# Thirty-six matmuls of a constant tile into an unused PSUM bank, at the head of a decoder layer

## The chip, the cores and the metric

The kernel runs on one NeuronCore of a Trainium2 chip. The metric is device time in microseconds of one execution, from the first to the last instruction with what lies around them. Five engines run their own instruction streams: PE (TensorE, matmuls; its weight loads are listed apart as PEld), DVE (VectorE), ACT (ScalarE), POOL (GpSimd) and SP, which here only issues DMAs.

## What is computed

One decoder layer over 512 tokens of width 1024, all in 32-bit floats: an RMS norm, one wide projection, two attention branches, a mixture of experts, an embedding gate and a final norm. Cut to what the change stands beside, the head of it:

```python
h = _rmsnorm(x, attn_norm[i])
proj = jnp.matmul(h, w_in[i])
q_a, c_kv, q_idx, k_idx, w_idx, qkv_b, gate_a, gate_b = _split_cols(proj)
...
rel = jax.nn.relu(jnp.einsum("bqhe,bse->bqhs", qi, k_idx))
score = jnp.einsum("bqhs,bqh->bqs", rel, wi)
_, idx = lax.top_k(score, n_sel)
...
x = x + jnp.matmul(merged, w_out[i])
x = x + _hier_moe(_rmsnorm(x, ffn_norm[i]), ...)
x = x + jnp.matmul(p[i], w_ple[i]) * jax.nn.sigmoid(jnp.matmul(_rmsnorm(x, ple_norm[i]), w_ple_gate[i]))
return _rmsnorm(x, final_norm)
```

## The kernel before

Tokens lie in four tiles `xs[0]` to `xs[3]` of 128 rows by 1024 columns. Each is loaded by one DMA from SP's queue (L102). ACT's queue loads `ident`, the 128x128 identity (L105), and then the norm gains, four small DMAs into the 32-row tile `norms` (L108 to L111). DVE fills `ones_r`, a 128x128 tile of ones, among its first instructions (L122).

PE's order is the order of the code, since PE is scheduled by hand; the other engines' orders come from a scheduler, and `pin` ties some instructions to the one traced ahead of them. PE's first instruction is a transpose of `norms` into bank 1 (`gains_ps`, L215). Meanwhile each x tile goes through ACT (sum of squares, L220), DVE and POOL (reciprocal root, L125 and L126) and DVE (scaling of the tile, L222).

Then x is turned: `turn_x(t, k)` (L232) transposes the 128x128 block k of tile t into column range t of bank `tps[k]`. For the first three tiles and k = 0 to 6 these are 21 transposes. The fourth tile is turned block by block inside `split_x(k)`: a transpose on PE, then ACT copies the bank, scaled by the gain, into the high half `hT_hi` (L132), and DVE writes the rest as `hT_lo` (L136). The last block, k = 7, has no bank of its own and follows when bank 2 has been read. High and low halves feed every projection as three matmuls (`mm3`, L80 to L82), first the key index `kidx_ps`, then the query index `qidx_ps`. Weights go through the same kind of split: POOL writes `whi` (L130), DVE `wlo` (L134).

PSUM has eight banks. `tps` takes 2, 3, 4, 5, 6, 7 and 0, in this order; bank 1 holds `gains_ps` and after it `kidx_ps`. Bank 0 is first written by the transposes of block 6.

The lines around the place of the change:

```python
gp_ = bank(1, "gains_ps")
nc.tensor.transpose(gp_[:, :32], norms, ident[:32, :32])
ss = cp.tile([P, 4], F32, name="ss1")
for t in range(NT):
...
for t in range(NT - 1):
    for k in range(len(tps)):
        turn_x(t, k)
wki = take("ki", ahead=0)
```

Of the kernel before, what the change touches and what calls it, by code (L numbers as in the profile page):

```python
# [18 lines left out]
P = 128  # L19
# [30 lines left out]
def hybrid_layer_kernel(ctx: ExitStack, tc: tile.TileContext, x, p, attn_norm, w_in, kv_norm, w_uk, w_uv,  # L50
                        rel_bias, w_branch_a, w_branch_b, w_out, ffn_norm, w_r1, b_r1, w_r2, b_r2,
                        w_gate, w_up, w_down, ple_norm, w_ple_gate, w_ple, final_norm, cst, out):
    nc = tc.nc
# [6 lines left out]
    def bank(i, name):  # L60
        return ps.tile([P, S], F32, tag=f"bank{i}", bufs=1, name=name)
# [59 lines left out]
    negtri, strict_r, ones_r = [cp.tile([P, P], F32R, name=n) for n in ("negtri", "strict_r", "ones_r")]  # L121
# [91 lines left out]

    gp_ = bank(1, "gains_ps")
    nc.tensor.transpose(gp_[:, :32], norms, ident[:32, :32])  # L215
    ss = cp.tile([P, 4], F32, name="ss1")
    for t in range(NT):
        xt = xs[t]
# [700 lines left out]
    for u in range(NT):  # L919
        n = NT - u  # L920
        nc.tensor.matmul(rkp[:, (u + 1) * NE:(NT + 1) * NE], ones_r, hits[:, u:u + 1, :].to_broadcast([P, n, NE]),
                         start=False, stop=u == NT - 1, skip_group_check=True)
# [360 lines left out]
```

## Time and profile before

| | us |
|---|---|
| median of 3 runs | 761.29 |
| lowest and highest of the 3 | 759.28, 762.74 |
| the profiled execution | 756.49 |
| its span, first to last instruction | 754.8 |
| PE busy in the span | 723.3 |

The profiled execution has 1.7 us around its span. Start times below are counted from the start of the span. A matmul's row starts where it starts and its end is modelled, so neighbours overlap: what one of a row of equal matmuls costs is the distance of the starts, that is the stretch of the row less one duration, divided by their number less one. In the rows `xT_ps` and its kin are tiles by the program's names, and `x21` is the number of instructions that a row merges.

### The profile page before, as it was taken

How to read it: one execution, taken by the hardware profiler on the slowest of the kernel's cores; microseconds unless marked ns; L12 is line 12 of the kernel's file. 1: busy time of each engine (PE TensorE's matmuls, PEld its weight loads, DVE VectorE, ACT ScalarE, POOL GpSimd, SP SyncE). 2: the span in 40 equal slices, each digit the busy share in tenths (PEclk: the TensorE clock that was granted, in tenths of full speed). 3: DMA queues.
4: the chain of work that ended last, by engine and by line, in shares of the span. 5: the costliest groups of instructions: out<-in, count | busy, mean ns of one | idle time of the engine just before them, and what ended most of it. 6: DMA issues, size and time to landing. Idle time of an engine off the chain costs nothing. (4 is left out here: it accounts for less than half of the span.)

```text
span 754.8 us, 10213 instructions
## 1 busy us (share of the span) xinstructions
PE 723.3 (96%) x3696; PEld 506.7 (67%) x3696; DVE 452.9 (60%) x896; ACT 292.1 (39%) x657; POOL 216.7 (29%) x255
## 2 busy tenths in 40 slices
PE   5999999989999999999999999999999999998995
PEld 3889987867778778788878645444544445444885
DVE  5689999997877756326553513544555445545534
ACT  5364435535667554332212423222322222233723
POOL 3212323354462535124530221000100000217732
PEclk9999999999999999999999999999999999999999
DMA  7345332322222222287955669999999999995002
GB/s 241 93 139 159 85 85 56 98 85 84 84 71 85 70 84 85 84 239 265 367 175 230 214 225 377 410 414 410 407 411 402 406 383 412 402 364 196 1 1 111
DMA packets 89259, 160.59 MB, mean 213 GB/s; under 512 B 13497, under 2 KB 56562, under 8 KB 85106
## 3 DMA queue, kind: packets, MB, share of 16 engines
q1 hardware_dynamic: 78384, 150.78, 54.8%
q10 hardware_dynamic: 8514, 4.89, 2.2%
q0 software_dynamic: 2304, 4.20, 1.6%
q8 instruction: 31, 0.51, 0.3%
q14 instruction: 26, 0.21, 0.1%
HBM read 154.08 MB, written 9.96 MB: 217 GB/s over the span
## 5 line engine op out<-in xcount | busy, mean ns | idle before, releaser
L1031 PE MATMUL gu_ps<-ew,xT 128*64 128x512 f32 x512 | 112.9, 593 | 1.4 <-PEq L1073 1.3
L130 POOL TENSOR_SCALAR whi<-wraw 128x1024 fp32r<-128x1024 f32 (+1 forms) x51 | 56.4, 1106 | 138.7 <-issue 29.7
L1068 DVE TENSOR_TENSOR x<-cmb_ps,x 128x512 f32<-128x512 f32 x128 | 81.0, 682 | 12.5 <-PE cmb_ps L1066 12.5
L1031 PEld LDWEIGHTS gu_ps<-ew,xT 128*64 128x64 f32 x512 | 36.8, 137 | 74.2 <-issue 72.8
L134 DVE TENSOR_TENSOR wlo<-wraw,whi 128x1024 fp32r<-128x1024 f32 (+1 forms) x51 | 64.7, 1269 | 14.8 <-POOL whi L130 14.8
L1007 POOL DMA_INDIRECT xg<-h_d,trow x16 | 16.1, 1008 | 186.3 <-PE cmb_ps L1065 170.9
L1035 DVE TENSOR_TENSOR hid<-hid,gu_ps 128x256 f32<-128x256 f32 x16 | 6.8, 422 | 104.4 <-ACT hid L1034 104.4
L1054 PE MATMUL yp<-ew,hidT 128*64 128x512 f32 x256 | 58.7, 599 | 0.4 <-DVE hidT L1044 0.4
L80 PE MATMUL gate_ps<-hT_hi,whi 128*128 128x512 f32 x128 | 51.9, 405 | 2.4 <-DVE ks L297 1.8
L1065 PE MATMUL cmb_ps<-yh,hotT 128*128 128x512 f32 x128 | 53.1, 415 | 0.4 <-DVE h3T L1152 0.4
L132 ACT ACTIVATE yh<-yp,sm 128x512 fp32r<-128x512 f32 x32 | 22.0, 687 | 79.2 <-PE yp L1054 79.2
L81 PE MATMUL gate_ps<-hT_lo,whi 128*128 128x512 f32 x128 | 50.8, 397 | 0.0
L82 PE MATMUL gate_ps<-hT_hi,wlo 128*128 128x512 f32 x128 | 50.7, 396 | 0.0
L1066 PE MATMUL cmb_ps<-yl,hotT 128*128 128x512 f32 x128 | 50.4, 394 | 0.3 <-DVE yl L136 0.3
L1034 ACT ACTIVATE hid<-gu_ps 128x256 f32<-128x256 f32 x16 | 6.1, 383 | 97.3 <-PE gu_ps L1031 97.3
L1054 PEld LDWEIGHTS yp<-ew,hidT 128*64 128x64 f32 x256 | 16.9, 136 | 33.0 <-issue 28.1
L136 DVE SCALAR_TENSOR_TENSOR yl<-yp,sm,yh 128x512 fp32r<-128x512 f32 x32 | 24.0, 750 | 21.1 <-ACT yh L132 21.1
L1019 ACT ACTIVATE xT<-xg_ps,gpm 128x128 f32<-128x128 f32 x128 | 34.7, 383 | 3.8 <-PE xg_ps L1016 3.8
L583 ACT ACTIVATE px<-px,st 128x128 f32<-128x128 f32 (+3 forms) x32 | 17.8, 557 | 36.6 <-DVE st L582 36.5
L80 PEld LDWEIGHTS gate_ps<-hT_hi,whi 128*128 128x128 f32 x128 | 24.3, 190 | 9.1 <-POOL bm L562 3.6
L1065 PEld LDWEIGHTS cmb_ps<-yh,hotT 128*128 128x128 f32 x128 | 24.1, 188 | 6.9 <-issue 2.4
L82 PEld LDWEIGHTS gate_ps<-hT_hi,wlo 128*128 128x128 f32 x128 | 24.5, 191 | 5.5
(328 smaller groups left out, 1760.6 us busy)
## 6 DMA issues: line engine op xcount, KB each, us to landing
ew<-in_w_gate_dram SPq DMA_DIRECT2D x32, 1024.0 KB, 8.1
ew<-in_w_up_dram SPq DMA_DIRECT2D x32, 1024.0 KB, 8.5
ew<-in_w_down_dram SPq DMA_DIRECT2D x32, 1024.0 KB, 7.5
wraw<-in_w_in_dram SPq DMA_DIRECT2D x37, 512.0 KB, 3.7
gate_d<-gst ACTq DMA_DIRECT2D x16, 256.0 KB, 2.0
sg<-gate_d SPq DMA_DIRECT2D x16, 256.0 KB, 4.4
wraw<-in_w_out_dram SPq DMA_DIRECT2D x8, 512.0 KB, 7.3
wgraw<-in_w_ple_gate_dram SPq DMA_DIRECT2D x4, 1024.0 KB, 9.4
```

Of the source, the lines that this page charges most:

```text
L80: nc.tensor.matmul(o, lhs[0], rhs[0], start=first, stop=False)
L81: nc.tensor.matmul(o, lhs[0], rhs[1], start=False, stop=False)
L82: nc.tensor.matmul(o, lhs[1], rhs[0], start=False, stop=last)
L130: hold(nc.gpsimd.tensor_scalar(hi, raw, 1.0 if gain is None else gain, 1.0, op0=ALU.mult, op1=ALU.mult))
L134: hold(V.tensor_sub(lo, raw, hi.bitcast(F32)))
L136: hold(V.scalar_tensor_tensor(lo, raw, gain, hi.bitcast(F32), op0=ALU.mult, op1=ALU.subtract))
L1019: nc.scalar.activation(xT[half][:, k, :], tp[:, k * P:(k + 1) * P], AF.Copy, scale=gpm[:, kk:kk + 1])
L1031: nc.tensor.matmul(gu_ps[64 * e:64 * e + 64, :], xT[k // 4][:, k % 4, 64 * e:64 * e + 64], wq[i, k // 4][:, :, e * D + (k % 4) * 256:e * D ...
L1054: nc.tensor.matmul(yp[64 * e:64 * e + 64, :], hidT[:, k, 64 * e:64 * e + 64], wq[i, 2][:, e, k * D + nh * S:k * D + (nh + 1) * S], start=k ...
L1065: nc.tensor.matmul(cp_, hT_[:, t * P:(t + 1) * P], yh, start=True, stop=False)
L1066: nc.tensor.matmul(cp_, hT_[:, t * P:(t + 1) * P], yl, start=False, stop=True)
L1068: V.tensor_add(xd, cp_, xd)
```

## The change

Behind the transpose of the gains, a tile `idle_ps` is taken in bank 0, and 36 matmuls are issued into its first 128 columns, each with the tile of ones as weights and as moving operand. Nothing reads `idle_ps`.

```diff
     gp_ = bank(1, "gains_ps")
     nc.tensor.transpose(gp_[:, :32], norms, ident[:32, :32])
+
+    idle_ps = bank(0, "idle_ps")
+    for _ in range(36):
+        nc.tensor.matmul(idle_ps[:, :P], ones_r, ones_r, start=True, stop=True)
     ss = cp.tile([P, 4], F32, name="ss1")
     for t in range(NT):
         xt = xs[t]
```

On PE, at its very start, the order of before and after differ by this (the names are tiles; line numbers behind the insertion grow by 4):

```order
 L215 MATMUL gains_ps<-cst_sb,norms 128x32
-L232 MATMUL xT_ps<-cst_sb,xt 128x128 x28
+L219 MATMUL idle_ps<-ones_r 128x128 x36
+L236 MATMUL xT_ps<-cst_sb,xt 128x128 x28
 L80 MATMUL kidx_ps<-hT_hi,whi 72x512
 L81 MATMUL kidx_ps<-hT_lo,whi 72x512
```

The 36 stand between the transpose of the gains and the first 28 transposes of x; nothing else on PE moves. The same place of after, with the semaphores that each instruction waits on (DMAHW ones belong to DMAs, the others to engines):

```order
L215 MATMUL gains_ps<-cst_sb,norms 128x32 [waits DMAHW4_49,DMAHW5_49,DMAHW3_49,DMAHW7_49,DMAHW1_49,DVE_49]
L219 MATMUL idle_ps<-ones_r 128x128 [waits DVE_49]
L219 MATMUL idle_ps<-ones_r 128x128 x35
L236 MATMUL xT_ps<-cst_sb,xt 128x128 [waits DVE_49]
L236 MATMUL xT_ps<-cst_sb,xt 128x128 x5
L236 MATMUL xT_ps<-cst_sb,xt 128x128 [waits PE_49]
```

The transpose of the gains waits on five DMAs in both kernels. The first of the 36 waits on DVE, for the tile of ones, and a seventh transpose of x now waits on PE itself, since bank 0 held `idle_ps`. The orders of ACT, DVE, POOL and SP are the same in both kernels, row for row.

## Rows read from the trace of the kernel before

**Rows 1.** The page: busy time, share of the span and instructions; PE's busy tenths by slice.
```profile
PE 723.3 (96%) x3696; PEld 506.7 (67%) x3696; DVE 452.9 (60%) x896; ACT 292.1 (39%) x657; POOL 216.7 (29%) x255
PE   5999999989999999999999999999999999998995
```

**Rows 2.** Timeline to 12.5 us: start, us, engine, line, operation, count [idle before, releaser].
```profile
1.18 0.17 DVE L122 MEMSET ones_r<- 128x128 f32 x1
2.49 0.36 ACTq L111 DMA_DIRECT2D norms<-in_ffn_norm_dram  x1
6.84 0.75 DVE L222 TENSOR_SCALAR xt<-xt,ss 128x1024 f32<-128x1024 f32 x1 [0.67 <-POOL ss L126]
7.65 0.28 PE L215 MATMUL gains_ps<-cst_sb,norms 32*128 32x32 f32 x1 [7.65 <-DVE xt L222]
7.86 3.83 PE L232 MATMUL xT_ps<-cst_sb,xt 128*128 128x128 f32 x21
11.29 1.17 DVE L222 TENSOR_SCALAR xt<-xt,ss 128x1024 f32<-128x1024 f32 x1 [0.66 <-POOL ss L126]
```

**Rows 3.** Timeline from 12.5 us: the fourth tile's transposes and what follows.
```profile
12.51 0.98 PE L232 MATMUL xT_ps<-cst_sb,xt 128*128 128x128 f32 x7 [0.82 <-DVE xt L222]
12.88 3.57 ACT L132 ACTIVATE hT_hi<-xT_ps,gains 128x512 fp32r<-128x512 f32 x6 [2.95 <-PE xT_ps L232]
13.60 2.73 DVE L136 SCALAR_TENSOR_TENSOR hT_lo<-xT_ps,gains,hT_hi 128x512 fp32r<-128x512 f32 x4 [0.39 <-ACT hT_hi L132]
...
17.37 2.72 DVE L136 SCALAR_TENSOR_TENSOR hT_lo<-xT_ps,gains,hT_hi 128x512 fp32r<-128x512 f32 x4
20.79 0.34 PE L80 MATMUL qidx_ps<-hT_hi,whi 128*128 128x384 f32 x1
```

**Rows 4.** Transposes before 10.6 us (timeline), and weight loads after it (by line).
```profile
8.13 2.56 PE L232 MATMUL xT_ps<-cst_sb,xt 128*128 128x128 f32 x11
L232 PEld LDWEIGHTS xT_ps<-cst_sb,xt 128*128 128x128 f32 x7 | 0.8, 141 | 0.0
```

**Rows 5.** Timeline of short fp32r matmuls at the higher clock, then one tile's instructions.
```profile
455.01 1.04 PE L990 MATMUL tabw<-vhl,hot 128*128 128x32 f32 x8
...
162.21 0.28 PE L526 MATMUL z_ps<-sl,negones 128*128 128x256 f32 x1
162.33 0.22 PE L526 MATMUL z_ps<-sh,negones 128*128 128x128 f32 x1
162.39 0.27 PE L526 MATMUL z_ps<-sl,negones 128*128 128x128 f32 x1
...
L990 PE MATMUL tabw<-vhl,hot x8: 262/262/263, 455.0 to 455.8; 128*128 128x32 f32 x8
```

**Rows 6.** Stretches: length, busy time by engine (PE, PEld, DVE, ACT, POOL), granted clock, DMA.
```profile
18.00:20.00 2.00, 1.83 (x8) 1.15 (x9) 2.00 (x4) 0.51 (x2) 0.00 (x0) 1.00 0.82 234
20.00:24.00 4.00, 4.00 (x24) 3.68 (x23) 2.30 (x5) 1.19 (x2) 1.05 (x1) 1.00 0.13 37
280.30:283.70 3.40, 3.40 (x10) 2.64 (x9) 0.62 (x2) 0.90 (x2) 0.29 (x1) 0.50 0.17 51
437.30:440.70 3.40, 3.40 (x5) 1.33 (x4) 1.12 (x4) 0.37 (x1) 2.04 (x2) 0.50 0.10 19
```

**Rows 7.** Timeline around 280 us: matmuls ahead of and in the lower clock.
```profile
279.78 0.39 PE L81 MATMUL gate_ps<-hT_lo,whi 128*128 128x512 f32 x1
280.01 0.40 PE L82 MATMUL gate_ps<-hT_hi,wlo 128*128 128x512 f32 x1
282.77 0.63 PE L80 MATMUL gate_ps<-hT_hi,whi 128*128 128x512 f32 x1
283.19 0.62 PE L81 MATMUL gate_ps<-hT_lo,whi 128*128 128x512 f32 x1
```

**Rows 8.** Waits of PE over the span: for whom, us in total, times, longest.
```profile
PE qb_ps L80 <- DVE ks L297: 2.4, 1, 2.4
PE gate_ps L80 <- DVE ks L297: 1.8, 1, 1.8
```

## The prediction

> **What bounds the kernel now.** I read the page first. PE is busy 723.3 of 754.8 us, and of the 40 slices only the first and the last are half empty, the one by the loading of x, the other by the final norm [rows 1]. So time lost at the head is not won back on an idle PE later: the longest waits of PE behind the head are 2.4 and 1.8 us, each for DVE's splits, which themselves hang on earlier PE results [rows 8]. Nothing behind the head keeps a time of its own. What is late at 20 us is late at the end.
>
> Then I read the head itself on the timeline. PE does nothing for 7.65 us; its first instruction is the transpose of the gains, and the first transpose of x follows at 7.86 [rows 2]. The row puts the wait on DVE's scaling of x tile 0, which ends at 6.84 + 0.75 = 7.59. The program says otherwise: that instruction waits on five DMAs (the identity and the gains), the last of them issued at 2.49 behind 2 MB of x, and on no x tile. The two ends fall together within 0.1 us, so for the sum it doesn't matter which; for the meaning of the change it does. PE's order is fixed. Whatever stands behind the gains' transpose starts at 7.86, not at 1.35, where the tile of ones is ready.
>
> From 7.86, 21 transposes of tiles 0 to 2 run to 7.86 + 3.83 = 11.69. Then PE waits 0.82 us for DVE's scaling of tile 3, which ends at 11.29 + 1.17 = 12.46, and turns tile 3 from 12.51 on [rows 2, 3]. From there a chain without slack begins: ACT's first `hT_hi` at 12.88, DVE's first `hT_lo` at 13.60, then DVE without a pause through four `hT_lo`, one `wlo` and four `hT_lo` to 17.37 + 2.72 = 20.09, then the query index on PE at 20.79 [rows 3]. DVE is full (2.00 of 2.00) from 18 to 20, and PE is full from 20 to 24 [rows 6]. So the start of tile 3's transposes, 12.51, sets the rest, and the cover ahead of it is what PE has left there.
>
> **The change part by part.** It adds 36 matmuls, with a weight load each (the page has as many weight loads as matmuls, 3696 [rows 1]), between the gains' transpose and the 21 transposes. It adds no work on other engines, no DMA, and their orders stay. The wait on PE's own bank 0 is for the last of the 36, which is long past by the seventh transpose: nothing.
>
> Cost of one of the 36. No row shows fp32r matmuls of 128 columns in a long row with 128x128 weights. The nearest at the higher clock is `tabw`: eight matmuls of 32 columns, each with a 128x128 load, in 1.04 us, 262 ns each; the starts are (1.04 - 0.262) / 7 = 0.111 us apart [rows 5]. With a quarter of the columns this distance isn't the columns': it is the load's. The transposes of x agree: seven loads of 128x128 in 0.8 us, 141 ns each, (0.8 - 0.14) / 6 = 0.11 us apart [rows 4]. A lower bound is a pair in the second branch: two fp32r matmuls of 128 columns start at 162.33 and 162.39, 0.06 us apart, but the load of the second can have gone ahead under the 256-column matmul before the pair [rows 5]. I take 0.111.
>
> At the start PE is slower. Eleven transposes from 8.13 take 2.56 us, and with 0.42 us for one the starts are (2.56 - 0.42) / 10 = 0.214 us apart, twice the 0.11 of later ones [rows 4]. So they ran at the lower of the clock's levels, 1.2 GHz, though the granted clock's column says 1.00 there; the same doubling stands at 280 us, where the column says 0.50 [rows 6] and the starts of 512-column matmuls go from 0.23 to 0.42 us apart [rows 7]. In this execution the rate changed at about 10.6 us, after 13 transposes: 7.86 + 13 x 0.214 = 10.64.
>
> Now the sum, if the clock rises at the same moment, since PE becomes busy at the same moment: 13 of the 36 at 0.214 to 10.64; the other 23 at 0.111, 2.55 us, to 13.19; the 21 transposes at 0.11, 2.31 us, to 15.50. Tile 3 starts at 15.50 instead of 12.51: **3.0 us late**. Crosscheck: 36 x 0.111 = 4.0 us more work, less the cover: the last of the 21 starts 0.27 us ahead of its end at 11.42, the next could have followed at 11.53, and 12.51 - 11.53 = 0.98 us is free. Again 3.0.
>
> No gain stands against it. The higher clock had already come ahead of the wait at 11.69; the transposes that ran at the lower one were not on the path, since tile 3 came later than all of them. DVE and ACT have nothing else to do meanwhile that would shorten the chain: `wlo` of the key index ends ahead of `hT_lo` in either case, the second `wlo` stands in DVE's order between the `hT_lo`, and POOL's next `whi`, for the second query tile, needs a buffer that the key index on PE gives back, and moves along.
>
> Bounds. With 0.06 at the higher clock and 0.12 at the lower, 23 of the 36 fit up to 10.6 and 13 x 0.06 = 0.78 us follow: 11.4 + 2.31 = 13.7, 1.2 us late. With the lower clock through all 57: 7.86 + 57 x 0.214 = 20.06, 7.5 us late. Between them, each us by which the clock rises later leaves 1 / 0.214 = 4.7 instructions done instead of 9, and costs 0.48 us: a rise 2 us later gives 4.0, 1 us earlier 2.5. Below nothing the price itself can't go: PE starts when it did, in a fixed order.
>
> The Trainium skill, TensorE: Matmul & The Clock Gate, section Back-to-back issue gap, gives 107 ns cold and 56 ns warm for 128 columns alone, and about 81 ns in a stream with weight loads. By it 25 of the 36 would be done at 10.6, and 11 x 0.081 = 0.9 us would follow: tile 3 at 13.8, 1.3 us late. The rows above speak against it for 32-bit operands: 0.11 us even for 32 columns.
>
> **The rivals.** *Cheap matmuls or an early start.* If repeated loads of the same tile can be fetched ahead, one costs 0.06, and 1.2 us are lost: 762.5. For it: the pair at 162 us. Against it: `tabw`. A gains DMA that lands 1.6 us sooner where no profiler runs would give as little, as PE would start sooner.
>
> *Slow clock.* If PE's rate stays at the lower level through most of the 57, they cost 4 to 7.5 us: 765.3 to 768.8. For it: I see one rise in one execution. Against it: the transposes kept PE no busier than the 36 would, and the rate rose within 3 us. It decides from a rise 1.7 us later than here (3.8 us, 0.5%).
>
> *Not slower.* PE falls to the lower clock twice later, for 3.4 us each, at about 280.3, soon after 1.8 us without work, and at 437.3 [rows 6, 8]. In 3.4 us eight matmuls go at 0.42 that take 0.23 each otherwise [rows 7]: 8 x 0.19 = 1.5 us each time. If PE's later course, moved by 3 us, meets neither fall, 3.0 us come back, and nothing is lost: 761.3. It decides from the second fall that goes; one of the two alone gives 762.8. For it: PE also stands still for 2.4 us elsewhere [rows 8] and the clock holds, so a pause of this length doesn't always bring a fall. Against it: the pauses stay as long as they are, and a moved course can meet a fall at another pause as well.
>
> *It does nothing for what it says.* It is to run while x is loaded; it runs behind the gains' DMA, when tile 0 is scaled already. This is in the forecast.
>
> **How the numbers follow.** The forecast has 60 in 100, cheap matmuls or an early start 15, the slow clock 17, not slower 8. The profiled execution would go from 756.49 to 759.5. That execution is faster than all three runs shown, by 4.8 us against their median, and I put the same 3.0 us on the median: 761.29 + 3.0 = 764.3, slower by 0.39%. The three runs span 3.5 us, so a median is uncertain by about 1 us. The range leaves out the ends of the slow clock and of the early start: 760.3 to 767.5. A measurement of this kernel can tell about 0.5%, 3.8 us, from no change. Slower by more takes the slow clock (17) and a part of the forecast whose rise comes later or whose median falls high (12): 0.29. Faster by more needs both later falls gone and a median that falls low: 0.03. The rest is 0.68.
>
> **What would show it.** Right: a row of 36 `idle_ps` from about 7.9 us, the first about 0.21 us apart and the last 0.11; the transposes of tiles 0 to 2 in a closed row behind them, with no wait ahead of tile 3's; tile 3's at about 15.5 and the first query index at about 23.8, both 3 us later; the rest of the trace moved by as much. Wrong: starts 0.06 us apart; PE starting well ahead of 7.6; the first query index near 21; a different number of stretches at 0.50 later on.

## The result, and the profile after

The changed kernel takes 763.89 us (median of 7 runs, 762.91 to 768.06) and the kernel before 759.31 us beside it (7 runs, 756.25 to 762.74). The difference is +4.6 us, the ratio 1.0074 with an interval from 1.0044 to 1.0103. The time is 0.4 us from the 764.3 that I gave, but two misses cancel in that. The base was 2.0 us lower in these runs than the 761.29 on which I put my 3.0, and the loss was 1.6 us larger (2.6 by the ratio, which is 5.6 us of 759.31). That the time came out so near is luck. By the bound of 0.5% the change is slower, on which I had put 0.29 against 0.68 for "within"; the interval reaches a little below the bound. It is no gain in any case. The profiled execution took 763.32 us, with a span of 761.6 (before 756.49 and 754.8).

The page of after, to be held against [rows 1]: PE has its 36 instructions more and 8.9 us more of busy time (its ends are modelled and overlap, so the busy time is no price), and the other engines what they had.

```profile
PE 732.2 (96%) x3732; PEld 515.3 (68%) x3732; DVE 453.1 (59%) x896; ACT 292.4 (38%) x657; POOL 217.0 (28%) x255
PE   6999999989999999999999999999999999999995
```

The timeline of after from 7.6 us answers [rows 2] and [rows 3] (start and length in us, engine, line, operation, count, in brackets the idle time before and its releaser):

```profile
7.60 0.28 PE L215 MATMUL gains_ps<-cst_sb,norms 32*128 32x32 f32 x1 [7.60 <-DMA norms<-in_ffn_norm_dram]
7.81 7.94 PE L219 MATMUL idle_ps<-ones_r 128*128 128x128 f32 x36
...
11.79 1.17 DVE L226 TENSOR_SCALAR xt<-xt,ss 128x1024 f32<-128x1024 f32 x1 [0.66 <-POOL ss L126]
...
15.55 4.39 PE L236 MATMUL xT_ps<-cst_sb,xt 128*128 128x128 f32 x28
19.32 4.16 ACT L132 ACTIVATE hT_hi<-xT_ps,gains 128x512 fp32r<-128x512 f32 x7 [8.38 <-PE xT_ps L236]
20.04 2.73 DVE L136 SCALAR_TENSOR_TENSOR hT_lo<-xT_ps,gains,hT_hi 128x512 fp32r<-128x512 f32 x4 [6.32 <-ACT hT_hi L132]
...
27.22 0.34 PE L80 MATMUL qidx_ps<-hT_hi,whi 128*128 128x384 f32 x1
```

Five things are to be seen here. The 36 start at 7.81, directly behind the transpose of the gains, which this row puts down to the gains' DMA and not to DVE's scaling. They run for 7.74 us, to 15.55. The 28 transposes follow in one closed row, and nothing waits for tile 3 any more: DVE had scaled it by 11.79 + 1.17 = 12.96. ACT and DVE stand for 8.38 and 6.32 us, waiting for PE. And the first query index is at 27.22, where it was 20.79 [rows 3]: 6.43 us later, not 3.0.

The price of one is read from the view of the tile `idle_ps` (durations of the shortest, median and longest in ns, first and last start):

```profile
L219 PEld LDWEIGHTS idle_ps<-ones_r x36: 288/333/333, 7.8 to 15.2; 128*128 128x128 f32 x36
L219 PE MATMUL idle_ps<-ones_r x36: 415/415/476, 7.8 to 15.3; 128*128 128x128 f32 x36
```

The starts are (7.94 - 0.415) / 35 = 0.215 us apart, and the durations are alike from the first to the last. So all 36 ran at the lower level of the clock, 1.2 GHz, and none at the 0.111 that I took for 23 of them. The transposes behind them began at the lower level too. Here are eleven of them from 15.55, nine from 18.69 and the last seven, which are tile 3's (timeline of after, cut at these places, so that the last two rows overlap):

```profile
15.55 2.54 PE L236 MATMUL xT_ps<-cst_sb,xt 128*128 128x128 f32 x11
...
18.69 1.15 PE L236 MATMUL xT_ps<-cst_sb,xt 128*128 128x128 f32 x9
...
19.01 0.93 PE L236 MATMUL xT_ps<-cst_sb,xt 128*128 128x128 f32 x7
```

The first eleven start (2.54 - 0.42) / 10 = 0.21 us apart, the nine from 18.69 (1.15 - 0.27) / 8 = 0.11. Between them, at 17.9 us, the clock rises to 2.4 GHz: 10.1 us after the first of the 36, and 2.4 us after the first transpose. I shall call this moment the rise; it is where the spacing of equal starts halves. The column of the granted clock doesn't show it, since it says 1.00 up to its first recorded change.

With that the head adds up. From 7.81 the 36 take 7.74 us; the 21 transposes of tiles 0 to 2 take 3.46 us, a part of them at the lower level, where my sum had 2.31; tile 3's begin at 19.01 instead of 12.51. From there to the query index it is 8.21 us, nearly as before (20.79 - 12.51 = 8.28).

### The profile page after: what moved, and what is told of

It reads as the page before. It is cut to its first block, busy times and chain, and to the rows that moved or that the text cites. A ratio compares the mean times of both kernels' runs of the same rounds, so it can differ in the third digit from the quotient of the medians.

```text
span 761.6 us, 10285 instructions
## 1 busy us (share of the span) xinstructions
PE 732.2 (96%) x3732; PEld 515.3 (68%) x3732; DVE 453.1 (59%) x896; ACT 292.4 (38%) x657; POOL 217.0 (28%) x255
## 5 line engine op out<-in xcount | busy, mean ns | idle before, releaser
L1072 DVE TENSOR_TENSOR x<-cmb_ps,x 128x512 f32<-128x512 f32 x128 | 81.0, 683 | 12.5 <-PE cmb_ps L1070 12.5
```

The costliest lines, as they stand in the source:

```text
L1072: V.tensor_add(xd, cp_, xd)
```

## The experiments

Three theories stood against each other. **A**: a row of fp32r matmuls of 128 columns, each with its 128x128 weight load, doesn't bring the higher clock, however long it is; the transposes of x do. **B**: the moment of the rise is chance, and this execution had a late one. **C**: it lies in the data, since a constant times a constant changes nothing in the array.

The table collects what the runs below showed in the head (us from the span's start; ratios against runs of the kernel before, taken beside them):

| kernel | PE's work from | rise | first query index | ratio |
|---|---|---|---|---|
| before | transposes 7.86 | 10.6 | 20.79 | 1 |
| before, second trace | transposes 7.85 | 11.7 | 23.29 | 1.0017 [0.9983, 1.0051] |
| before, third trace | transposes 7.69 | 12.3 | 23.25 | one run |
| after | 36 at 7.81, transposes 15.55 | 17.9 | 27.22 | 1.0074 [1.0044, 1.0103] |
| after again | 36 at 7.47, transposes 15.21 | 20.4 | 28.06 | 1.0066 [1.0035, 1.0097] |
| varied data | 36 at 7.79, transposes 15.53 | 19.0 | 27.73 | 1.0064 [1.0039, 1.0090] |
| 12 in place of 36 | 12 at 7.83, transposes 10.45 | 12.3 | 21.86 | 0.9986 [0.9957, 1.0014] |
| 72 in place of 36 | 72 at 7.77, transposes 23.19 | 25.3 | 34.73 | 1.0173 [1.0135, 1.0212] |
| 36 ahead of the gains | 36 at 1.40, transposes 9.52 | 12.2 | 22.67 | 0.9978 [0.9947, 1.0009] |
| 36 plain float32 | 72 passes at 7.82, transposes 18.36 | 12.9 | 28.85 | 1.0059 [1.0025, 1.0093] |
| 9 of 512 columns | 9 at 7.83, transposes 11.84 | 12.45 | 22.97 | 0.9996 [0.9969, 1.0022] |
| 14 of 512 columns ahead of the gains | 14 at 1.94, transposes 8.06 | 5.55 | 23.54 | 0.9982 [0.9955, 1.0009] |
| tiles 2 and 3 in one DMA | transposes 7.75 | 12.9 | 21.97 | 1.0029 [1.0005, 1.0054] |
| the same with the 36 | 36 at 7.92, transposes 15.66 | 20.45 | 28.49 | 1.0057 [1.0029, 1.0086] |

**The same kernel again.** The edit is none. It asks whether the rise comes late a second time.

> The changed kernel once more, for a second look at when the clock rises. [...] Theory B (the moment of the rise is chance and has nothing to do with what the 36 are): the doubling falls anywhere from 2 to 10 us after PE's first instruction, and here most likely elsewhere than in the first look; tile 3 at 14.5 to 19. [...]

It took 763.02 us against 758.61. In the timeline the 36 again take 7.74 us, all at the lower level, and the transposes behind them begin at it:

```profile
7.47 7.94 PE L219 MATMUL idle_ps<-ones_r 128*128 128x128 f32 x36
15.21 5.78 PE L236 MATMUL xT_ps<-cst_sb,xt 128*128 128x128 f32 x28
...
28.06 0.33 PE L80 MATMUL qidx_ps<-hT_hi,whi 128*128 128x384 f32 x1
```

The rise is at 20.4, 5.2 us after the first transpose. How long the transposes need varies (2.4 us in the first trace); that the 36 didn't bring the rise is the same in both.

**The same 36 in plain float32.** Only the type is changed. Each matmul reads the same tile, for both operands, and writes the same place.

```diff
+    ones_f = ones_r.bitcast(F32)
-        nc.tensor.matmul(idle_ps[:, :P], ones_r, ones_r, start=True, stop=True)
+        nc.tensor.matmul(idle_ps[:, :P], ones_f, ones_f, start=True, stop=True)
```

> The same 36 at the same place, with operands read as plain float32 in place of float32r; a plain 512-column matmul of this kernel takes 0.42 us at the higher clock, 128 columns 0.107, so columns stream nearly all the time, as in the transposes. Theory A: the clock rises 2 to 4 us after the first of the 36, and tile 3 starts at 15 to 16.5 us; 2.5 to 4 us slower than before, about 3 us faster than the changed kernel's first look. Theory B: no difference to the changed kernel that goes one way. Theory C: as the changed kernel, all 36 at 0.214 us, tile 3 at 18.5 to 19.5.

It took 764.26 us against 758.61. The rise now comes in the middle of the idle matmuls (timeline, one row of them whole and then in two pieces around the rise):

```profile
7.82 10.70 PE L220 MATMUL idle_ps<-ones_r 128*128 128x128 f32 x72
...
7.82 5.06 PE L220 MATMUL idle_ps<-ones_r 128*128 128x128 f32 x22
13.00 5.41 PE L220 MATMUL idle_ps<-ones_r 128*128 128x128 f32 x47
18.36 3.22 PE L237 MATMUL xT_ps<-cst_sb,xt 128*128 128x128 f32 x28
```

The first 22 start (5.06 - 0.42) / 21 = 0.22 us apart, the 47 from 13.00 (5.41 - 0.275) / 46 = 0.112. So 5.05 us after the first of them the clock rose, at 12.87, while they were running; through the 36 fp32r ones it stayed low for 7.7 us. The price was mis-sized in my expectation: plain float32 makes two instructions of each matmul, 72 for 36. So this run speaks on the clock and not on the cost. It also rules out that one tile as both operands, or one place written over and over, keeps the clock low, since both are so here too.

**The same columns in wide matmuls.** Nine of 512 columns stream as many columns as 36 of 128, with nine loads in place of 36.

```diff
-    for _ in range(36):
-        nc.tensor.matmul(idle_ps[:, :P], ones_r, ones_r, start=True, stop=True)
+    wide_r = hT[1][:, KD - 1, :]
+    V.memset(wide_r.bitcast(F32), 1.0)
+    for _ in range(9):
+        nc.tensor.matmul(idle_ps, ones_r, wide_r, start=True, stop=True)
```

> The same number of columns in nine matmuls of 512 columns in place of 36 of 128, float32r, ones as weights and as moving operand (a row of h's low half, not yet in use, is filled with ones by one more DVE instruction in DVE's idle head). Nine at 0.427 us at the lower level or 0.23 at the higher. [...] Theory B: rise anywhere. Theory C: the nine take 3.84 us to 11.65, the transposes go on at 0.214 us until 2 to 4 us of them have run, tile 3 at 14.5 to 15.5.

It took 757.98 us against 758.61, the same as before. From the timeline:

```profile
7.83 4.21 PE L221 MATMUL idle_ps<-hT_lo,ones_r 128*128 128x512 f32 x9
11.84 3.58 PE L238 MATMUL xT_ps<-cst_sb,xt 128*128 128x128 f32 x28
```

Nine take 11.84 - 7.83 = 4.0 us, 0.446 each, at the lower level; the rise is at 12.45, 4.6 us after the first of them and 0.6 us after the first of the transposes behind them. So it can't be put down to the nine alone; the run with fourteen below shows it while wide ones run. A quarter of 0.446 is 0.111: by this estimate the columns of one of the 36 take half of its 0.215 us, and the rest would be the weight load's, which no run here shows by itself. The first query index is at 22.97, between those of the three traces of the kernel before.

**Varied data.** The tile holds 16 different values instead of ones, for both operands.

```diff
+    mixed_r = hT[1][:, KD - 1, :P]
+    for i in range(16):
+        V.memset(mixed_r.bitcast(F32)[:, 8 * i:8 * i + 8], math.sin(1.0 + 7.3 * i) * 2.0 ** (i % 7))
-        nc.tensor.matmul(idle_ps[:, :P], ones_r, ones_r, start=True, stop=True)
+        nc.tensor.matmul(idle_ps[:, :P], mixed_r, mixed_r, start=True, stop=True)
```

> The 36 as in the changed kernel (float32r, 128 columns), but with a tile of 16 different values, eight columns each, in place of ones, for both operands. Theory A: nothing changes, all 36 at 0.214 us, tile 3 at 18.5 to 19.5. Theory B: rise anywhere. Theory C: the clock rises 2 to 4 us after the first of the 36, tile 3 starts at 15 to 16.5 us, 3 us faster than the changed kernel.

It took 762.25 us against 758.61. The timeline reads as that of after:

```profile
7.79 7.94 PE L222 MATMUL idle_ps<-hT_lo 128*128 128x128 f32 x36
15.53 4.92 PE L239 MATMUL xT_ps<-cst_sb,xt 128*128 128x128 f32 x28
```

The rise is at 19.0. Theory C falls, as far as 16 values go.

**The kernel before, a second and a third time.** My cover of 0.98 us was read from one execution, and these runs ask how far it holds. The edit is that the four new lines are gone.

> The kernel before once more, for a second look at when its clock rises without the 36. [...] Theory B (the rise is chance): the doubling may come as late as 18 to 20 us here, and the key index then goes at half rate, with the query index at 24 or later.

> The kernel before, a third look at its head. Two looks gave tile 3's transposes at 12.5 and 14.5 us and the first query index at 20.8 and 23.3. If the landing of tile 3 varies from one execution to the next, this one lies between or near either; a start of the query index well above 23.5 or below 20.5 would be against it.

The times were 761.72 against 760.27, and a single run of 758.98. The second trace, from its timeline and from its stretches (length, busy time of PE, PEld, DVE, ACT, POOL, granted clock, DMA):

```profile
7.85 4.36 PE L232 MATMUL xT_ps<-cst_sb,xt 128*128 128x128 f32 x21
11.28 1.06 ACT L220 ACTIVATE junk<-xt 128x1024 f32<-128x1024 f32 x1 [2.65 <-DMA xt<-in_x_dram]
13.28 1.17 DVE L222 TENSOR_SCALAR xt<-xt,ss 128x1024 f32<-128x1024 f32 x1 [0.66 <-POOL ss L126]
14.50 1.24 PE L232 MATMUL xT_ps<-cst_sb,xt 128*128 128x128 f32 x7 [2.30 <-DVE xt L222]
...
15.10:18.50 3.40, 3.11 (x10) 1.51 (x9) 3.40 (x5) 3.40 (x7) 0.25 (x1) 0.50 0.42 103
```

Tile 3 landed later (ACT waits 2.65 us for its DMA), PE waits 2.30 us for it instead of 0.82 [rows 3], and then the clock falls to 0.50 for 3.4 us, under the matmuls of the key index. The third trace has the same two marks:

```profile
13.88 0.99 PE L232 MATMUL xT_ps<-cst_sb,xt 128*128 128x128 f32 x7 [1.47 <-DVE xt L222]
...
15.70:19.10 3.40, 3.05 (x10) 2.09 (x10) 3.40 (x6) 2.71 (x5) 0.00 (x0) 0.50 0.60 154
23.25 0.34 PE L80 MATMUL qidx_ps<-hT_hi,whi 128*128 128x384 f32 x1
```

So the execution on which I predicted was an early one. Its query index is at 20.79, the other two have 23.29 and 23.25; the mean is 22.4. From tile 3 to the query index it takes 8.28 us without the fall and 8.79 and 9.37 with it (8.2 to 8.6 in the traces of the other kernels that have no such fall). The three traces with 36 in place (after, again, varied data) have 27.22, 28.06 and 27.73, a mean of 27.7. The head loses 27.67 - 22.44 = 5.2 us. The three measured differences are 4.6, 4.4 and 3.6 us by the medians (after, after again, varied data) and 5.6, 5.0 and 4.9 by the ratios. With three traces on each side, which spread over 2.5 and 0.8 us, that agrees to 1 or 2 us and no better.

**The 36 ahead of the gains' transpose.** They need only the tile of ones, so in this place they start early, and PE is busy while x is loaded.

```diff
+    idle_ps = bank(0, "idle_ps")
+    for _ in range(36):
+        nc.tensor.matmul(idle_ps[:, :P], ones_r, ones_r, start=True, stop=True)
     gp_ = bank(1, "gains_ps")
     nc.tensor.transpose(gp_[:, :32], norms, ident[:32, :32])
```

> The same 36 float32r matmuls of 128 columns, but ahead of the gains' transpose, so that they can run from 1.5 us on while x is really being loaded. Theory A: the clock stays low through them, 36 x 0.214 = 7.7 us from 1.5 to 9.2 us; the gains' transpose and the first transposes of x come 1.5 us later than before, the 21 go at 0.214 until 2 to 5 us after 9.4, and tile 3 starts at 13.0 to 14.0 us: 0 to 1.5 us slower than before. If the 36 do raise the clock: they end ahead of 7 us, the transposes start at 7.9 us at 0.11 each and all is hidden, 0 against before.

It took 758.97 us against 760.27. The timeline:

```profile
1.40 7.94 PE L216 MATMUL idle_ps<-ones_r 128*128 128x128 f32 x36 [1.40 <-DVE ones_r L122]
9.28 0.31 PE L218 MATMUL gains_ps<-cst_sb,norms 32*128 32x32 f32 x1
9.52 3.79 PE L235 MATMUL xT_ps<-cst_sb,xt 128*128 128x128 f32 x21
14.09 0.98 PE L235 MATMUL xT_ps<-cst_sb,xt 128*128 128x128 f32 x7 [0.78 <-DVE xt L225]
```

The same instructions cost nothing here, as tile 3's transposes still wait 0.78 us for DVE behind them. So the loss is one of place. The clock stays low through all 36 again, and rises 2.7 us after the first transpose; as a means to raise it, they fail in this place as well.

**Wide matmuls ahead of the gains' transpose.** This was to be the version that does what the change seems to be after, a clock that is high when x arrives.

```diff
+    idle_ps = bank(0, "idle_ps")
+    wide_r = hT[1][:, KD - 1, :]
+    V.memset(wide_r.bitcast(F32), 1.0)
+    for _ in range(14):
+        nc.tensor.matmul(idle_ps, ones_r, wide_r, start=True, stop=True)
     gp_ = bank(1, "gains_ps")
     nc.tensor.transpose(gp_[:, :32], norms, ident[:32, :32])
```

> Fourteen float32r matmuls of 512 columns ahead of the gains' transpose, ones as weights and moving operand (one more DVE instruction fills the ones). Theory A: they begin at about 2 us, the clock rises 2 to 5 us later, they end by 7.5 us, the transposes run at 0.11 us from their first on, tile 3 starts when DVE has scaled it and not later than before; the clock is up in every execution when the key index begins. 0 to 2 us faster than before, and 4 to 6 us faster than the changed kernel. Theory B: they end at 8 us at the latest and change nothing on average.

It took 758.49 us against 760.27; the interval reaches from 0.45% faster to 0.09% slower, so no difference from before is shown. The timeline, seven and six of the 14 on either side of the rise, the transposes, and a stretch behind them:

```profile
1.94 3.35 PE L218 MATMUL idle_ps<-hT_lo,ones_r 128*128 128x512 f32 x7 [1.94 <-DVE hT_lo L216]
...
5.52 1.59 PE L218 MATMUL idle_ps<-hT_lo,ones_r 128*128 128x512 f32 x6
...
8.06 2.10 PE L237 MATMUL xT_ps<-cst_sb,xt 128*128 128x128 f32 x14
...
14.40 0.98 PE L237 MATMUL xT_ps<-cst_sb,xt 128*128 128x128 f32 x7 [2.76 <-DVE xt L227]
...
15.80:19.20 3.40, 2.95 (x9) 1.67 (x9) 3.40 (x6) 3.13 (x6) 0.00 (x0) 0.50 0.57 154
```

The spacing goes from (3.35 - 0.63) / 6 = 0.45 to (1.59 - 0.39) / 5 = 0.24: the clock rises at 5.55, and the first transposes of x run at the higher level. It buys nothing that the runs can tell. PE then waits 2.76 us for tile 3, at 14.40, and the clock falls behind that wait (the stretch from 15.80, granted clock 0.50), so that the first matmuls of the key index run at the lower level, where I had expected the higher. In this execution what sets the head is when tile 3 lands, not how fast PE turns tiles 0 to 2.

**Twelve in place.** It measures the cover by itself.

```diff
-    for _ in range(36):
+    for _ in range(12):
```

> Twelve of the 36 in place. Theory A, with the clock low through them: 12 x 0.214 = 2.6 us, the transposes start at 10.4 us and go at 0.214 until 2 to 5 us of them have run; the 21 end at 13.6 to 14.9 us, and tile 3 starts then, 1.1 to 2.4 us later than in the profile of before; by time 1 to 2.5 us slower than before. By the forecast's own price (13 at 0.214, the rest at 0.111, the rise at 10.6): 1.3 us less the cover of 0.98, 0.4 us.

It took 759.37 us against 760.27. In the timeline the twelve go from 7.83 to 10.45:

```profile
7.83 2.82 PE L219 MATMUL idle_ps<-ones_r 128*128 128x128 f32 x12
10.45 4.13 PE L236 MATMUL xT_ps<-cst_sb,xt 128*128 128x128 f32 x28
...
13.65 0.93 PE L236 MATMUL xT_ps<-cst_sb,xt 128*128 128x128 f32 x7
```

They push the transposes back by 2.6 us, and nothing of it shows in the time: the interval ends at 0.14% slower, or 1.1 us, and I had expected 1 to 2.5. That expectation was reckoned from the early execution of before. Tile 3's transposes start at 13.65 here, without a wait, which lies between the 12.51 and 14.50 of the three traces of before; against the later two the 2.6 us are hidden by the cover.

**Seventy-two in place.** It measures the price without the cover, which the first 36 have used up.

```diff
-    for _ in range(36):
+    for _ in range(72):
```

> Seventy-two in place of 36, at the same place. The cover is used up by the first 36, so the second 36 show the price of one without it. Theory A (the clock stays low through all of them): 36 x 0.214 = 7.7 us more than the changed kernel; the 72 run to 23.3 us, tile 3 starts at 26 to 27.5, the first query index at 34.5 to 36; 11.5 to 13.5 us slower than before. By the forecast's price at the higher clock: 36 x 0.111 = 4.0 us more, 8 to 9 us slower than before.

It took 774.47 us against 759.72. The timeline, with the transposes in two pieces:

```profile
7.77 15.62 PE L219 MATMUL idle_ps<-ones_r 128*128 128x128 f32 x72
23.19 2.29 PE L236 MATMUL xT_ps<-cst_sb,xt 128*128 128x128 f32 x10
25.13 2.33 PE L236 MATMUL xT_ps<-cst_sb,xt 128*128 128x128 f32 x19
...
34.73 0.34 PE L80 MATMUL qidx_ps<-hT_hi,whi 128*128 128x384 f32 x1
```

For 15.4 us PE does nothing but these matmuls, and every one is 0.214 us from the next. The transposes begin at (2.29 - 0.42) / 9 = 0.21 us apart and end at (2.33 - 0.27) / 18 = 0.11; the rise is at 25.3. By the ratios the second 36 cost 1.0173 - 1.0074 = 1.0%, 7.5 us, but the intervals of the two make that uncertain by some 4 us; the trace is sharper, with the query index 34.73 - 27.22 = 7.5 us later. 36 x 0.214 = 7.7. At my 0.111 the second 36 would have cost 4.0.

**Two x tiles in one DMA, without and with the 36.** If tiles 2 and 3 come in one transfer, I thought, tile 3 is no longer late, and there is no cover.

```diff
-    xin = tc.alloc_tile_pool(name="xin", bufs=4, side="right")
+    xin = tc.alloc_tile_pool(name="xin", bufs=2, side="right")
-    for t in range(NT):
+    for t in range(2):
+    both = xin.tile([P, 2, D], F32, tag="xt23", bufs=1, name="xt23")
+    nc.sync.dma_start(both, x[0, 2 * P:, :].rearrange("(t p) d -> p t d", p=P))
+    xs += [both[:, 0, :], both[:, 1, :]]
```

> The kernel before, without the 36, with tiles 2 and 3 of x loaded by one DMA in place of two, so that the load of tile 3 no longer waits in SP's queue for tile 0 to land. Theory D (tile 3's landing, which came anywhere from 8.7 to 11.2 us in the traces so far, sets when the head's chain begins, and so how much of the 36 is covered): tile 3 is scaled at 12.3 to 13 us in every execution, its transposes start then, the first query index at 20.7 to 21.5; 1 to 2.5 us faster than before. If the landing doesn't matter, or the larger load delays tile 2 as much: within 0.5 us of before.

> The same with the 36 in place. Theory D with theory A: the cover is smaller than in the changed kernel, while the 36 and the transposes still end at 18.5 to 20 us; the time is that of the changed kernel within 1 us (763 where before is 758.6), and 5.5 to 7.5 us slower than the run with one DMA and without the 36. If the 36 cost what the forecast said: 3 to 4 us slower than that run.

Without the 36 it took 760.65 us against 759.76, ratio 1.0029 [1.0005, 1.0054]: the gain that I expected didn't come. Tile 3's transposes start at 13.42 after a wait of 0.24 us, but tile 2 comes later than in before, and the query index is at 21.97, inside the spread of the three traces of before. With the 36 it took 764.56, ratio 1.0057 [1.0029, 1.0086], 3.9 us above the same without them by the medians and about 2 by the ratios. Its traced execution took 770.23 us, the longest of the twelve, so that its row in the table is used for the place of the rise alone. I expected 5.5 to 7.5 with the cover gone. The wait moved to another tile rather than vanished, so this pair doesn't isolate the cover; it is inconclusive on that.

## Why the prediction was right and wrong

**Place and order: right.** PE starts behind the gains' DMA at 7.6 us, the 36 follow at once, the transposes close up behind them without a wait for tile 3, and the chain from tile 3 to the query index keeps its length (8.21 us for 8.28). The 36 run beside nothing that they could hide behind but the wait for tile 3. That they stand in the wrong place is shown by the run that has them ahead of the gains' transpose, without loss.

**The price: wrong.** The step that failed is "if the clock rises at the same moment, since PE becomes busy at the same moment", and with it 13 at 0.214 and 23 at 0.111. That gives 5.3 us; the 36 took 7.74, all at the lower level, and the 21 transposes took 3.46 us for the 2.31 that I had, since the rise came only after them or among them. 7.74 - 5.33 = 2.4 and 3.46 - 2.31 = 1.1 are the 3.5 us between tile 3's 15.50 of the sum and 19.01 in the trace. That was my rival of the slow clock, at 17 in 100 and 4 to 7.5 us, and the measured loss lies in it and not in the forecast. I held against it that transposes keep PE no busier than the 36 would. The runs show that it is the kind of matmul that differs. In the seven traces with fp32r matmuls of 128 columns at the start (after, the same again, the varied data, the 36 ahead of the gains, the 72, the 36 behind the joined DMA, and the 12, which are too few to tell much) the clock stayed low to the end of them and rose 1.8 to 5.2 us after the transposes had begun. With transposes, plain float32 or 512 columns at the start it rose 2.7 to 5.2 us after the first. As far as these traces go, theory B falls with that, C with the varied data, and A holds. Neither the type nor the number of columns does it alone: plain float32 of 128 columns and fp32r of 512 columns both had the rise while they ran. Why the clock tells the kinds apart is not shown by these runs.

On the single price, the Trainium skill (TensorE: Matmul & The Clock Gate, section Back-to-back issue gap) gives N / 1.2 ns as the gap of single matmuls of N columns at the lower clock, which is 107 ns for 128. The 36, each with a weight load, stand 0.215 us apart in the trace, twice that; the measurement decides. My rival of cheap matmuls falls in its price at the lower clock, 0.12. Its 0.06 at the higher clock, and my own 0.111, stay open, since no run here has a row of these matmuls at the higher clock.

**The cover: wrong, in the other direction.** I took 0.98 us from one execution with an early tile 3. In the two other traces of the kernel before PE waits 2.30 and 1.47 us, and then loses another 0.5 and 1.1 us to a fall of the clock, which none of the traces with a closed row of transposes and no such wait has. "No gain stands against it" was too narrow: in these executions the filled pause gives the fall back. The head of after is 6.43 us later than that of the early execution, but 5.2 us later in the mean of three against three. In sum, for the first query index: the forecast's 3.0, 3.4 more in the first trace of after, above all for the price (6.43 - 3.0), 0.45 more in the mean of the three (27.67 for 27.22), less the 1.65 us by which the mean of the three traces of before, 22.44, lies behind 20.79: 5.2.

**One to one to the end: right for 330 us, then not quite.** Instruction by instruction, PE in after is 6.43 us late from the query index to 150 us, and 8.02 from 173 us on, as there is a third fall of the clock that before does not have [rows 6]:

```profile
171.50:174.90 3.40, 3.29 (x8) 2.65 (x9) 3.33 (x7) 1.36 (x4) 2.73 (x4) 0.50 0.00 0
```

The first of the `tabw` matmuls, at 455.0 in [rows 5], is 7.5 us late in after and 5.7 in the repeat of it:

```profile
L994 PE MATMUL tabw<-vhl,hot x8: 262/262/263, 462.5 to 463.3; 128*128 128x32 f32 x8
```

```profile
L994 PE MATMUL tabw<-vhl,hot x8: 262/263/263, 460.7 to 461.4; 128*128 128x32 f32 x8
```

In the repeat PE is 7.24 us late up to 325 us; between 330 and 391 us 1.6 of that comes back. PE waits there for DVE's splits of weights 1.2 us in before, and 0.2 in the repeat, so 1.0 of the 1.6 is such a wait that takes up the lateness; the rest I can't place. So "nothing behind the head keeps a time of its own" was too strong. Another 1.0 comes back in both at 681 us of before, where PE waited for its own sequencer. Here is that row in the waits of before, and then in those of after (for whom, us in total, times, longest):

```profile
PE gu_ps L1031 <- PEq L1073: 1.3, 1, 1.3
```

```profile
PE gu_ps L1035 <- PEq L1077: 0.4, 1, 0.4
```

This isn't one execution's luck: the same wait is 1.3, 1.0 and 1.4 us in the three traces of before, and 0.4, 0.3 and 0.3 in the three with the 36 in place. It doesn't shrink with the lateness, though, as the 72 have 2.1 and the plain float32 2.6; what sets it stays open. At the end after is 6.84 us late, the repeat 4.72, each against the one early execution of before. The mean span of the three traces with the 36 (761.6, 759.5, 761.8) is 4.0 us above that of the three of before (754.8, 758.7, 757.3), so some 1.2 of the 5.2 us of the head don't reach the end.

**Not slower: wrong.** The falls of the clock later in the span do vary. Without the one at the end of every span, before shows two and the other traces of it three or four, after three and its repeat two, each about 1.6 us. They make part of the scatter of the runs and no trend in favour of the change.

**A version that beats both: none.** The four variants that cost nothing (12 or nine wide ones in place, 36 or fourteen wide ones ahead of the gains) are, by the ratios, 0.8 to 1.0% faster than the changed kernel and not measurably faster than the one before.

## What to carry to other kernels

Filler work on an engine with a fixed order starts when the instruction ahead of it may start, not when its own operands are ready; look at what that one waits for, and place the filler ahead of it if the time to be filled lies there. Price it at the lower clock unless a trace shows this kind of matmul at the higher one, and count the weight load of each: 36 small ones cost 7.7 us here and warmed nothing, while nine wide ones with as many columns in all took 4.0. And read the cover, which is a difference of two arrival times, from several executions: here it was 0.8, 1.5 and 2.3 us in three.

## What the runs showed of the hardware

The clock stayed at 1.2 GHz through 15.4 us in which PE ran 72 fp32r matmuls of 128 columns without a gap, each with a weight load, and rose 2.1 us after transposes followed. With fp32r matmuls of 512 columns it rose while they ran, 3.6 us after the first. A plain float32 matmul of 128 columns stands in the trace as two instructions, so 36 made 72, each 0.22 us apart at the lower clock and 0.112 at the higher.

A pause of PE of 2.30, 1.47 or 2.76 us in the head was followed by 3.4 us at half the clock (the second and third traces of before, and the wide matmuls ahead of the gains), while a pause of 0.82 us was not [rows 3]. The length of the pause alone doesn't settle it: PE's wait of 2.4 us for `qb_ps` [rows 8] ended at 171.6 us in after, with the fall at 171.5, and at 167.7 us in the second trace of before, with a fall at 168.7, while in before, in its third trace and in the repeat of after the same wait had no fall near it. And the granted clock's column reads 1.00 ahead of its first recorded change, though the spacing of the starts says half: at the start of a span, go by the starts.
